# Gated delta rule of a hybrid encoder trunk: substitution through the two 64-row halves of a block in place of one joined inverse

## The chip, the cores and the metric

The kernel runs on one core of a Trainium2 chip. The metric is the device time of one launch in microseconds (us), smaller being better. TensorE multiplies matrices, VectorE and ScalarE work element by element and empty the accumulators (PSUM), GpSimd does a few small operations, and SyncE issues the loads.

## What is computed

Two layers run over 256 positions of width 1024. Each has a gated feed-forward half-step, a mixing stage and a second feed-forward half-step, each followed by a normalisation. The mixing stage projects its input once (`w_in`), runs three groups of heads side by side (differential attention, Mamba-2, gated delta rule) and merges them with one output projection (`w_out`). The change lies in the delta rule, whose core is this part of the reference:

```python
lmat = jnp.where(strict, jnp.einsum('bhcld,bhcsd->bhcls', kb, kc) * decay, 0.0)
imat = jnp.eye(CHUNK, dtype=jnp.float32) + lmat
u = lax.linalg.triangular_solve(imat, vb, left_side=True, lower=True, unit_diagonal=True)
w = lax.linalg.triangular_solve(imat, kb * jnp.exp(gc)[..., None], left_side=True, ...)
...
def step(st, inp):
    u_i, w_i, qd_i, kd_i, a_i, dec_i = inp
    v_new = u_i - jnp.einsum('bhld,bhdv->bhlv', w_i, st)
    o_i = jnp.einsum('bhld,bhdv->bhlv', qd_i, st) + jnp.einsum('bhls,bhsv->bhlv', a_i, v_new)
    st = st * dec_i[..., None, None] + jnp.einsum('bhld,bhlv->bhdv', kd_i, v_new)
    return st, o_i
```

So `v_new` solves a unit lower triangular system. The kernel takes blocks of 128 rows (two of the reference's chunks of 64), so for each of 4 heads and 2 blocks there is one 128 by 128 system, made of two triangles of 64 by 64 on the diagonal and a full 64 by 64 square below them.

## The kernel before

**Tiling.** The 256 positions are two blocks `b` of 128. The large products (feed-forward, `w_in`, `w_out`) split each fp32 operand into a high and a low part and use three TensorE products (lines 221, 222, 228 or 224, and 301). A weight unit is loaded by SyncE into one of 5 `raw` buffers, ScalarE casts the high part (`wh`, line 232), VectorE subtracts for the low part (`wl`, line 233), and 7 `wh` and 7 `wl` buffers hold units ahead of the products. The `w_out` units add into `po`, for `b` = 0 and 1 separately.

**What sets the order.** The program is written out by a planner: `run` emits the weight products one by one, and after each one calls `step`, which advances every generator ("chain") whose due time lies behind the planner's clock. A `yield 0.8` in a chain sets how long it waits, in the planner's estimate, before its next piece is emitted. Each engine then works through its own instructions in the emitted order and waits on semaphores; so a longer or shorter chain moves its neighbours on every engine.

**The delta rule.** `delta` (line 605) forms `LA` for each block: the scaled triangle of keys against keys, and queries against keys. `inverse` (line 743) builds the inverses of the two 64-row triangles of all 8 (block, head) pairs at once, in five levels of block size 2 to 32, kept transposed in `TT` (`T` is the untransposed copy, `gps` and `ups` are the PSUM tiles of a level's two products, `G` the masked copy between). At the last level it also brings `T` up to date for the first half (lines 789 to 793). Then it joins the halves: `X` holds, for the second 64 rows of the result, the columns of the whole inverse; its lower part is copied from `TT` (796), its upper part is made by two further products with a copy between (799 to 808). Back in `delta`, `rhs` is the right side (line 666), and for `b` = 0 and then `b` = 1 eight products into `vnps` give `vnew` (702 to 707): per head one of 64 by 64 for the first half, one over all 128 rows with `X` for the second. From `vnew` come the state `S` (`sps`, only `b` = 0) and the outputs (`ops`). For `b` = 1, `rps` (`S` against keys and queries) first corrects `rhs` (line 685).

**What stands around it.** The Mamba-2 chain (`after_m11`, `after_mz`) runs at the same time: `yps`, `yfps`, then `y` (lines 875 to 908), its squares `msq` on ScalarE (912), the reciprocal root on GpSimd (394, 396), the scaling of `y` on VectorE (920), and transposes into `mTps` on TensorE, which feed the third to sixth `w_out` unit. The delta rule's output `go` takes a similar way (squares 726, sum 728, root, scaling 734, 736) to the last transposes `mTps<-cst,go`, which feed the last two units. The first two units need only the attention's output.

Of the kernel before, what the change touches and what calls it, by code (L numbers as in the profile page):

```python
# [13 lines left out]
ALU = mybir.AluOpType  # L14
# [77 lines left out]
class Kernel:  # L92
# [512 lines left out]
    def delta(self, l, qk, sq):  # L605
        nc = self.nc
        ve = nc.vector
# [22 lines left out]
        LA = []  # L630
# [28 lines left out]
        pk = self.aux(0, "ktok")  # L659
        self.transposes([qk[:, 0, 0:P], qk[:, 2, 0:P]], pk)  # L660
        ve.tensor_tensor(x4, pk[:, 0:256].rearrange("p (h d) -> p h d", h=4), b4(de), op=ALU.mult)
        TT, X = yield from self.inverse(LA)
        lo, hi = slice(0, 64), slice(64, P)
        yield from self.until("gv")
        rhs = self.w([8, 64], "rhs")
# [6 lines left out]
        for b in range(2):  # L672
            if b == 1:

                pr = [self.aux(b, "rps") for _ in range(2)]
                for a in range(2):
                    for j in range(2):
                        for p in range(2):
                            o = slice(64 * p, 64 * p + 64)
                            at = 128 * a + 64 * j  # L680
                            self.mm(pr[p][:, at : at + 64], lhsT=qk[o, 2 * j + a, blk(1)], rhs=S[o, j, :])
                for p in range(2):
                    for j in range(2):
                        hd = 2 * j + p
                        ve.scalar_tensor_tensor(
                            rhs[:, 4 + hd],
                            in0=pr[p][:, 64 * j : 64 * j + 64],
                            scalar=ne[:, hd : hd + 1],
                            in1=rhs[:, 4 + hd],
                            op0=ALU.mult,  # L690
                            op1=ALU.add,
                        )
                for p in range(2):
                    ve.tensor_tensor(
                        oS[:, p::2, :],
                        pr[p][:, 128:256].rearrange("p (j d) -> p j d", j=2),
                        ecs[:, 1, p:4:2].unsqueeze(2).to_broadcast([P, 2, 64]),
                        op=ALU.mult,
                    )
                yield 1.8  # L700
            vnew = self.h(b, [4, 64], "vnew")
            pn = self.aux(b, "vnps")
            for hd in range(4):
                e, c = 4 * b + hd, slice(64 * hd, 64 * hd + 64)
                self.mm(pn[lo, c], lhsT=TT[lo, e, :], rhs=rhs[lo, e, :])
                self.mm(pn[hi, c], lhsT=X[:, e, :], rhs=rhs[:, e, :])
            nc.scalar.copy(vnew.rearrange("p h d -> p (h d)"), pn[:, 0:256])
            yield 0.8
            if b == 0:
                pS = self.aux(b, "sps")  # L710
                for hd in range(4):
                    o = slice(64 * (hd % 2), 64 * (hd % 2) + 64)
                    j = hd // 2
                    self.mm(pS[o, 64 * j : 64 * j + 64], lhsT=x4[:, hd, :], rhs=vnew[:, hd, :])
                nc.scalar.copy(S.rearrange("p j d -> p (j d)"), pS[:, 0:P])
            po = self.aux(b, "ops")
            for hd in range(4):
                self.mm(po[:, 64 * hd : 64 * hd + 64], lhsT=LA[b][:, hd % 2, hd // 2, 1, :], rhs=vnew[:, hd, :])
            out = go[:, 4 * b : 4 * b + 4]
            if b == 0:  # L720
                nc.scalar.copy(out.rearrange("p h d -> p (h d)"), po[:, 0:256])
                yield 0.5
            else:
                ve.tensor_tensor(out, po[:, 0:256].rearrange("p (h d) -> p h d", h=4), oS, op=ALU.add)
# [18 lines left out]
    def inverse(self, LA):  # L743
# [20 lines left out]
        for n, s in enumerate(LEVELS):  # L764
# [21 lines left out]
            for e in range(8):  # L786
                for o in (lo, hi):
                    self.mm(pu[o, 32 * e : 32 * e + 32], lhsT=G[o, e, :], rhs=col1(TT[o, e, :], 1))
            if s == 32:
                for e in range(8):  # L790
                    self.mm(pu[lo, 256 + 32 * e : 288 + 32 * e], lhsT=TT[lo, e, :], rhs=G[lo, e, 0:32])
                dT = pu[lo, 256:512].rearrange("p (h s) -> p h s", h=8)
                ve.tensor_tensor(T[lo, :, 0:32], T[lo, :, 0:32], dT, op=ALU.subtract)
            ve.tensor_tensor(cols(TT, 1), cols(TT, 1), view(pu[:, 0:256]), op=ALU.subtract)
        X = self.w([8, 64], "X")
        nc.scalar.copy(flat(X[hi]), flat(TT[hi]))
        yield 1.2

        pg = self.aux(0, "gps")
        for e in range(8):  # L800
            self.mm(pg[hi, 64 * e : 64 * e + 64], lhsT=LT(e)[lo, hi], rhs=T[lo, e, :])
        G = self.w([8, 64], "G")
        nc.scalar.copy(G[hi].rearrange("p h s -> p (h s)"), pg[hi, :])
        yield 0.8
        pu = self.aux(0, "ups")
        for e in range(8):
            self.mm(pu[lo, 64 * e : 64 * e + 64], lhsT=G[hi, e, :], rhs=TT[hi, e, :])
        ve.tensor_scalar(X[lo], pu[lo, :].rearrange("p (h s) -> p h s", h=8), -1.0, None, op0=ALU.mult)
        yield 0.8
        return TT, X  # L810

    def after_m00(self, l, ps):
        self.xsT = self.big([4, 256], "xsT")
# [403 lines left out]
```

## Time and profile before

| | |
|---|---|
| median of 3 runs | 1095.92 us (1094.84 to 1097.18) |
| the profiled execution | 1094.49 us, span of its instructions 1092.7 us |
| TensorE | busy 1052.6 us, 96% of the span; granted clock 0.996 |
| VectorE, ScalarE, GpSimd | 759.1 us (69%), 600.2 us (55%), 42.0 us (4%) |
| loads | 184.99 MB, mean 169 GB/s |

Columns of the views: a timeline row has the start within the span, the duration, engine, line and operation, result and operands, shapes, and in brackets how long the engine sat idle before it and what released it. A TensorE product of fp32 operands appears as two instructions. TensorE works in a pipeline, so the durations of neighbouring rows overlap: the time that a product takes of the engine is read from start to start. The chain of waits lists, in order of time, the work that ended last at each step; its TensorE pieces are already cut so that they don't overlap. The mixing stages of the two layers lie 536.5 us apart and look alike; the first one is read.

### The profile page before, as it was taken

What the parts mean: (1) busy time and instruction counts of PE and PEld (TensorE: products, weight loads), DVE (VectorE), ACT (ScalarE), POOL (GpSimd) and SP (SyncE); (2) the same over time, 40 slices, a digit from 0 to 9 for tenths busy, and PEclk for the clock granted to TensorE, in tenths of its full rate; (3) what the DMA queues carried; (4) which work ended last, traced back from release to release, by engine and by line L of the source; (5) the groups of instructions that cost most, each with busy time, mean ns of one, the idle gap of its engine ahead of it and who ended that gap; (6) DMA issues with size and microseconds to landing.
All of it is one profiled execution on the core that took longest, in us unless ns stands there. A gap on an engine that the chain in (4) does not pass through costs nothing.

```text
span 1092.7 us, 17702 instructions
## 1 busy us (share of the span) xinstructions
PE 1052.6 (96%) x6397; PEld 896.7 (82%) x6397; DVE 759.1 (69%) x1531; ACT 600.2 (55%) x1284; POOL 42.0 (4%) x51
## 2 busy tenths in 40 slices
PE   6999999999998999999999999999989999999996
PEld 5888878788887788888878888877878877888885
DVE  5767754886867877774587776467967688777644
ACT  6677643487543566664346665436764345666530
POOL 0000000001001100000000000000010110000001
PEclk9999999999999999999999999999999999999999
DMA  9977665661234776666477666637513258666641
GB/s 289 255 210 203 197 195 144 174 193 40 72 104 140 206 214 193 191 188 196 139 225 207 188 193 191 193 98 206 161 40 98 89 159 245 185 192 193 194 134 39
DMA packets 222351, 184.99 MB, mean 169 GB/s; under 512 B 15160, under 2 KB 201912, under 8 KB 222264
## 3 DMA queue, kind: packets, MB, share of 16 engines
q1 hardware_dynamic: 222264, 183.87, 56.9%
q8 instruction: 50, 0.82, 0.3%
q14 instruction: 37, 0.30, 0.1%
HBM read 182.78 MB, written 1.05 MB: 168 GB/s over the span
## 4 chain that ended last, share of the span: by engine, by line
PE 79%; DVE 11%; ACT 3%; DMA 3%; issue 2%; POOL 2%; SPq 0%; DVEq 0%; POOLq 0%; ACTq 0%
PE ps L301 39%; PE po L221 7%; PE po L222 7%; PE po L228 7%; DVE wl L233 4%; PE ps L221 4%; PE ps L222 4%; PE ps L228 3%; DMA raw<-in_ffn_w_gu_dram 2%; PE ups L355 1%; PE gps L355 1%; DMA raw<-in_w_in_dram 1%; ACT wh L232 1%; POOL rsq L396 1%; PE vnps L355 1%
## 5 line engine op out<-in xcount | busy, mean ns | idle before, releaser
L233 DVE TENSOR_TENSOR wl<-raw,wh 128x512 fp32r<-128x512 f32 (+1 forms) x672 | 437.8, 682 | 191.9 <-ACT wh L232 185.3
L232 ACT CAST wh<-raw 128x512 fp32r<-128x512 f32 (+1 forms) x672 | 386.5, 615 | 205.8 <-PE po L228 99.7
L301 PE MATMUL ps<-xT,wh 128*128 128x512 f32 (+1 forms) x1600 | 484.8, 363 | 0.0
L301 PE MATMUL ps<-xT,wl 128*128 128x256 f32 x1376 | 388.4, 282 | 0.0
L301 PEld LDWEIGHTS ps<-xT,wh 128*128 128x128 f32 x1600 | 285.3, 188 | 48.6 <-issue 1.1
L301 PEld LDWEIGHTS ps<-xT,wl 128*128 128x128 f32 x1376 | 260.5, 189 | 0.7 <-issue 0.5
L221 PE MATMUL po<-wh,hT 128*128 128x512 f32 x352 | 137.7, 391 | 0.8 <-DVE hh L457 0.8
L222 PE MATMUL po<-wl,hT 128*128 128x512 f32 x352 | 137.1, 389 | 0.0
L228 PE MATMUL po<-wh,hT 128*128 128x512 f32 x336 | 103.5, 389 | 0.0
L221 PE MATMUL ps<-wh,xT 128*128 128x512 f32 (+2 forms) x256 | 97.1, 379 | 4.3 <-ACT wh L232 4.2
L222 PE MATMUL ps<-wl,xT 128*128 128x512 f32 (+2 forms) x256 | 94.6, 371 | 0.0
L228 PE MATMUL ps<-wh,xT 128*128 128x512 f32 (+2 forms) x224 | 83.6, 374 | 3.4 <-DVE xT L233 3.4
L221 PEld LDWEIGHTS po<-wh,hT 128*128 128x128 f32 x352 | 66.1, 188 | 15.7 <-DVE hh L457 2.2
L222 PEld LDWEIGHTS po<-wl,hT 128*128 128x128 f32 x352 | 66.1, 188 | 13.4
L228 PEld LDWEIGHTS po<-wh,hT 128*128 128x128 f32 x336 | 63.1, 188 | 13.2
L232 ACT CAST hT<-hh 128x256 fp32r<-128x256 f32 x72 | 29.2, 406 | 71.9 <-DVE hh L459 71.9
L221 PEld LDWEIGHTS ps<-wh,xT 128*128 128x128 f32 x256 | 48.5, 190 | 13.6 <-ACT wh L232 5.0
L222 PEld LDWEIGHTS ps<-wl,xT 128*128 128x128 f32 x256 | 48.6, 190 | 8.3 <-DVE wl L233 0.6
L458 ACT ACTIVATE ga<-ga 128x256 f32<-128x256 f32 x72 | 30.1, 418 | 42.4 <-DVE ga L455 42.2
L228 PEld LDWEIGHTS ps<-wh,xT 128*128 128x128 f32 x224 | 42.4, 189 | 11.1 <-DVE xT L233 4.2
L233 DVE TENSOR_TENSOR hT<-hh,hT 128x256 fp32r<-128x256 f32 x72 | 30.5, 424 | 25.8 <-ACT hT L232 25.6
L394 POOL TENSOR_SCALAR rs<-mv 128x1 f32<-128x1 f32 x12 | 6.3, 526 | 790.9 <-DVE mv L378 790.9
(233 smaller groups left out, 970.9 us busy)
## 6 DMA issues: line engine op xcount, KB each, us to landing
raw<-in_ffn_w_gu_dram SPq DMA_DIRECT2D x352, 256.0 KB, 3.5
raw<-in_ffn_w_down_dram SPq DMA_DIRECT2D x88, 512.0 KB, 3.5
raw<-in_w_in_dram SPq DMA_DIRECT2D x40, 512.0 KB, 3.8
raw<-in_w_out_dram SPq DMA_DIRECT2D x16, 512.0 KB, 3.5
raw<-in_w_in_dram SPq DMA_DIRECT2D x24, 256.0 KB, 3.9
g<-in_ln_g_dram SPq DMA_DIRECT2D x6, 512.0 KB, 5.5
b<-in_ln_b_dram SPq DMA_DIRECT2D x6, 512.0 KB, 5.6
x<-in_x_dram SPq DMA_DIRECT2D x4, 256.0 KB, 3.4
```

The source lines that it names most:

```text
L221: mm(p, lhsT=xh, rhs=wh, start=start, stop=False)
L222: mm(p, lhsT=xh, rhs=wl, start=False, stop=False)
L228: mm(p, lhsT=xl, rhs=wh, start=False, stop=False)
L232: self.nc.scalar.copy(hi, src)
L233: self.nc.vector.tensor_tensor(lo, src, hi.bitcast(F32), op=ALU.subtract)
L301: self.nc.tensor.matmul(to, lhsT=a, rhs=r, start=first and n == 0, stop=end and n == len(mms) - 1, skip_group_check=True,)
L355: self.nc.tensor.matmul(out, lhsT=lhsT, rhs=rhs, start=start, stop=stop)
L394: nc.gpsimd.tensor_scalar(t, ap, mul, add, op0=ALU.mult, op1=ALU.add)
L396: nc.gpsimd.tensor_tensor(r, t, self.neghalf[:, :n], op=ALU.pow)
L458: nc.scalar.activation(a, a, AF.Silu)
```

## The change

`inverse` stops at `TT`. The update of `T` at the last level and everything on `X` are gone: per layer 8 products into `ups`, 8 into `gps`, 8 into `ups`, two VectorE and two ScalarE operations, and three yields. In `delta` each block's eight products and one copy become three groups of four products of 64 by 64, with a step on another engine after each: first half from `TT`, copied to `vnew[lo]` by ScalarE; the square `LA[lo, hi]` against that, subtracted from `rhs[hi]` by VectorE; second half from `TT`, copied to `vnew[hi]` by ScalarE.

```diff
-        TT, X = yield from self.inverse(LA)
+        TT = yield from self.inverse(LA)
...
-            for hd in range(4):
-                e, c = 4 * b + hd, slice(64 * hd, 64 * hd + 64)
+            flat = lambda t, o: t[o].rearrange("p h d -> p (h d)")
+            heads = [(hd, 4 * b + hd, slice(64 * hd, 64 * hd + 64)) for hd in range(4)]
+            for hd, e, c in heads:
                 self.mm(pn[lo, c], lhsT=TT[lo, e, :], rhs=rhs[lo, e, :])
-                self.mm(pn[hi, c], lhsT=X[:, e, :], rhs=rhs[:, e, :])
-            nc.scalar.copy(vnew.rearrange("p h d -> p (h d)"), pn[:, 0:256])
+            nc.scalar.copy(flat(vnew, lo), pn[lo, 0:256])
+            yield 0.8
+            pn = self.aux(b, "vnps")
+            for hd, e, c in heads:
+                self.mm(pn[hi, c], lhsT=LA[b][lo, hd % 2, hd // 2, 0, hi], rhs=vnew[lo, hd, :])
+            r2 = rhs[hi, 4 * b : 4 * b + 4, :]
+            ve.tensor_tensor(r2, r2, pn[hi, 0:256].rearrange("p (h d) -> p h d", h=4), op=ALU.subtract)
+            yield 0.8
+            pn = self.aux(b, "vnps")
+            for hd, e, c in heads:
+                self.mm(pn[hi, c], lhsT=TT[hi, e, :], rhs=rhs[hi, e, :])
+            nc.scalar.copy(flat(vnew, hi), pn[hi, 0:256])
             yield 0.8
...
-            if s == 32:
-                for e in range(8):
-                    self.mm(pu[lo, 256 + 32 * e : 288 + 32 * e], lhsT=TT[lo, e, :], rhs=G[lo, e, 0:32])
-                dT = pu[lo, 256:512].rearrange("p (h s) -> p h s", h=8)
-                ve.tensor_tensor(T[lo, :, 0:32], T[lo, :, 0:32], dT, op=ALU.subtract)
             ve.tensor_tensor(cols(TT, 1), cols(TT, 1), view(pu[:, 0:256]), op=ALU.subtract)
-        X = self.w([8, 64], "X")
-        nc.scalar.copy(flat(X[hi]), flat(TT[hi]))
-        yield 1.2
-
-        pg = self.aux(0, "gps")
-        for e in range(8):
-            self.mm(pg[hi, 64 * e : 64 * e + 64], lhsT=LT(e)[lo, hi], rhs=T[lo, e, :])
-        G = self.w([8, 64], "G")
-        nc.scalar.copy(G[hi].rearrange("p h s -> p (h s)"), pg[hi, :])
-        yield 0.8
-        pu = self.aux(0, "ups")
-        for e in range(8):
-            self.mm(pu[lo, 64 * e : 64 * e + 64], lhsT=G[hi, e, :], rhs=TT[hi, e, :])
-        ve.tensor_scalar(X[lo], pu[lo, :].rearrange("p (h s) -> p h s", h=8), -1.0, None, op0=ALU.mult)
-        yield 0.8
-        return TT, X
+        return TT
```

Since the yields change, the planner emits other work around the delta rule. On every engine the instructions up to the last level's `ups` products and from the first block's normalisation on stand as before. The first group of block 0 now stands 9 weight products behind the last `ups`, the second behind `cbps`, the third 30 weight products later; `yps` and `yfps` follow behind it. `rhs<-gv,nk` on VectorE moves ahead of a `wl` step.

TensorE, second block, before: the last pair of `vnps` products, then the output products `ops`, then the first `w_out` product (`po`); `ps` is the projection's last part.

```order
L355 MATMUL vnps_3575<-rhs_3479,TT_2849 64x64
L355 MATMUL vnps_3575<-rhs_3479,X_3385 64x64
L222 MATMUL ps_3634<-wl_3410,xT_2107 128x256
L228 MATMUL ps_3634<-wh_3409,xT_2107 128x256
L221 MATMUL ps_3634<-wh_3409,xT_2107 128x256
L222 MATMUL ps_3634<-wl_3410,xT_2107 128x256
L355 MATMUL ops_3617<-vnew_3574,LA_2818 128x64 x4
L228 MATMUL ps_3634<-wh_3409,xT_2107 128x256
L221 MATMUL ps_3634<-wh_3409,xT_2107 128x256
L222 MATMUL ps_3634<-wl_3410,xT_2107 128x256
L224 MATMUL ps_3634<-wh_3409,xT_2107 128x256
L221 MATMUL po_3710<-wh_3471,mT_2490 128x512
```

TensorE, second block, now: the end of the first group, four weight products, the second group.

```order
L355 MATMUL vnps_3528<-rhs_3376,TT_2849 64x64 x3
L222 MATMUL ps_3618<-wl_3413,xT_2107 128x256
L228 MATMUL ps_3618<-wh_3412,xT_2107 128x256
L221 MATMUL ps_3618<-wh_3412,xT_2107 128x256
L222 MATMUL ps_3618<-wl_3413,xT_2107 128x256
L355 MATMUL vnps_3542<-vnew_3527,LA_2818 64x64 x4
L228 MATMUL ps_3618<-wh_3412,xT_2107 128x256
```

TensorE, second block, now, seven weight products later: the third group and `ops`.

```order
L224 MATMUL ps_3618<-wh_3412,xT_2107 128x256
L221 MATMUL po_3694<-wh_3455,mT_2490 128x512
L355 MATMUL vnps_3563<-rhs_3376,TT_2849 64x64 x4
L222 MATMUL po_3694<-wl_3456,mT_2490 128x512
L221 MATMUL po_3695<-wh_3455,mT_2490 128x512
L222 MATMUL po_3695<-wl_3456,mT_2490 128x512
L228 MATMUL po_3694<-wh_3455,mT_2490 128x512
L355 MATMUL ops_3601<-vnew_3527,LA_2818 128x64 x4
```

The third group and `ops` now stand behind the first `w_out` products; the last transposes `mTps<-cst,go` have 38 `w_out` products ahead of them where they had 33.

ScalarE, second block, before: from the copy of `go` of block 0 to the squares of `y`.

```order
L721 COPY go_3483<-ops_3515 128x256
L707 COPY vnew_3574<-vnps_3575 128x256
L912 ACTIVATE msq_3587,mss_3585<-y_3428 128x256
L912 ACTIVATE msq_3589,mss_3585<-y_3428 128x256
L912 ACTIVATE msq_3592,mss_3585<-y_3428 128x256
L912 ACTIVATE msq_3594,mss_3585<-y_3428 128x256
L726 ACTIVATE sq_616_3623<-go_3483 128x512
```

ScalarE, second block, now (lines 707 and 718 are the copies of the two halves).

```order
L232 CAST wh_3717<-raw_3461 128x512 x2
L707 COPY vnew_3527<-vnps_3528 64x256
L232 CAST wh_3752<-raw_3525 128x512
L718 COPY vnew_3527<-vnps_3563 64x256
L232 CAST wh_3752<-raw_3525 128x512
L903 ACTIVATE msq_3571,mss_3569<-y_3438 128x256
```

The squares stand behind both copies of the block and behind the two halves of one weight unit's cast, which stood behind them before. On VectorE the second block's subtraction (line 713) stands between the `yfps` step of `y` and the two operations that finish `y`.

## Rows read from the trace of the kernel before

**Rows 1.** Page, part 1: busy time (share), instructions, of TensorE.

```profile
PE 1052.6 (96%) x6397; PEld 896.7 (82%) x6397; DVE 759.1 (69%) x1531; ACT 600.2 (55%) x1284; POOL 42.0 (4%) x51
```

**Rows 2.** Waits of TensorE, whole run: us in total, times, longest.

```profile
PE xps L237 <- DVE x L383: 3.4, 4, 1.1
...
PE mTps L237 <- DVE y L920: 3.2, 2, 1.6
PE mTps L237 <- DVE go L736: 3.1, 2, 1.6
```

**Rows 3.** Windows of 4 us: length, busy per engine, clock, DMA share, GB/s.

```profile
336.00:340.00 4.00, 2.42 (x16) 2.10 (x16) 3.97 (x8) 1.40 (x3) 1.23 (x1) 1.00 0.41 131
344.00:348.00 4.00, 2.44 (x13) 1.95 (x13) 4.00 (x8) 1.45 (x3) 0.00 (x0) 1.00 0.17 51
348.00:352.00 4.00, 4.00 (x20) 3.29 (x19) 2.54 (x6) 1.03 (x3) 0.00 (x0) 1.00 0.99 311
```

**Rows 4.** Chain that ended last, first layer: start us, us, what.

```profile
300.32 1.05 PE ups L355 x32
...
308.10 1.98 PE ups L355 x48
...
312.98 1.07 PE gps L355 x16
...
316.27 0.84 PE ups L355 x12
...
318.14 0.37 PE ups L355 x4
...
322.65 2.05 PE vnps L355 x16
...
329.30 0.51 PE vnps L355 x4
...
330.36 1.55 PE vnps L355 x12
```

**Rows 5.** The same chain, from the squares of y to the last transposes.

```profile
332.21 1.72 ACT msq L912 x8
...
336.03 2.66 DVE y L920 x4
...
345.78 0.63 PE mTps L237 x4
```

**Rows 6.** Timeline of TensorE: start us, us, line, operation [idle before].

```profile
331.57 0.33 PE L355 MATMUL vnps<-rhs,X 128*64 128x64 f32 x2
331.83 0.39 PE L222 MATMUL ps<-wl,xT 128*128 128x256 f32 x1
...
332.40 1.06 PE L355 MATMUL ops<-vnew,LA 128*128 128x64 f32 x8
333.28 0.37 PE L228 MATMUL ps<-wh,xT 128*128 128x256 f32 x1
...
333.84 0.39 PE L221 MATMUL po<-wh,mT 128*128 128x512 f32 x1
334.07 0.39 PE L222 MATMUL po<-wl,mT 128*128 128x512 f32 x1
...
337.65 0.41 PE L237 MATMUL mTps<-cst,y 128*128 128x128 f32 x2 [1.58 <-DVE y L920]
```

**Rows 7.** Timeline of ScalarE, same columns.

```profile
331.94 0.37 ACT L707 COPY vnew<-vnps 128x256 f32<-128x256 f32 x1 [4.35 <-PE vnps L355]
...
335.09 1.14 ACT L232 CAST wh<-raw 128x512 fp32r<-128x512 f32 x2
```

**Rows 8.** Timeline of VectorE, same columns.

```profile
310.11 0.41 DVE L793 TENSOR_TENSOR T<-T,ups 64x256 f32<-64x256 f32 x1 [1.82 <-PE ups L355]
...
313.36 2.49 DVE L868 TENSOR_TENSOR ex<-ex,CB 128x512 f32<-128x512 f32 x4
...
329.60 1.28 DVE L908 TENSOR_TENSOR y<-y,sz 128x512 f32<-128x512 f32 x2
```

## The prediction

> **What bounds the kernel now.** I read the page's first part, then the waits of TensorE, the windows of the mixing stage, and last its chain of waits. TensorE is busy 96% of the span [rows 1], so by default an instruction taken off it is worth its own time. The exceptions are the places where it waits. Over both layers the transposes of `y` wait 3.2 us and those of `go` 3.1 us, two waits each, or 1.6 us per layer and place; each normalisation costs 1.1 us at most [rows 2]. The windows around the first two have only 2.4 of 4 us busy on TensorE, at full granted clock, and the next window is full again [rows 3]. The chain names what is late there: the second block's `vnps` products, then ScalarE's squares of `y`, GpSimd's root, VectorE's scaling of `y`, and from there to the transposes of `go` [rows 4, 5]. So the stage has two limits: up to the second block's `vnew` TensorE's own work, behind it a chain over four engines. Time taken off TensorE moves the start of that chain, and only that is won.
>
> **The change, part by part.** All for one layer; the other repeats it.
>
> *Removed from TensorE.* The last level's `ups` pieces take 1.98 us for 48 instructions, where a level without the update of `T` takes 1.05 us for 32: 0.93 us goes. The join's `gps` takes 1.07 us, its `ups` 0.84 + 0.37 us, the two blocks' `vnps` 2.05 and 0.51 + 1.55 us [rows 4]. Sum 7.32 us.
>
> *Added to TensorE.* Six groups of four 64 by 64 products, eight instructions each. The nearest row is the join's `gps`, the same shape, all products out of one half: 1.07 us for 16, 0.067 us each [rows 4], so 0.53 us a group and 3.2 us in all. From below it is bounded by `ups`, where the halves alternate: 1.05 us for 32, 0.26 us a group [rows 4]; from above by today's `vnps`, 2.05 us for 16, 0.128 us each, 1.03 us a group [rows 4]. I take 0.53, since shape and half agree. Net, TensorE gets rid of 4.1 us, with bounds of 1.1 and 5.7.
>
> Why do today's `vnps` instructions cost twice as much as those of `gps`? In them a 64-row product and a 128-row one alternate, in `gps` all have one shape [rows 4, 6]. The Trainium skill, TensorEngine Tiling (Array Packing), section Tiling Modes, says that a change of tiling mode drains the engine. That agrees with the row and would let the alternation's cost go; but it speaks against the change as well, because six short groups each enter and leave the small mode between full products. By the rule the difference of 0.061 us per instruction, some 0.12 us per change of mode, would come twice per group, 1.5 us a layer, and the sum would be some 3 us less for the whole kernel. The first full product behind `ops` starts its neighbour no earlier than today, so I keep the row's price.
>
> *Added waits.* Each group is followed by a step on another engine on which the next depends. Such a hand-over is in the trace: the last `vnps` pair starts at 331.57 us and `ops`, behind the copy, at 332.40: 0.83 us [rows 6]. Four weight products of 256 columns that stand between take 332.40 - 331.83 = 0.57 us [rows 6]. In the second block again four stand between first and second group, so TensorE waits about 0.26 us. Between second and third stand seven and one of 512 columns, over 1 us, between third and `ops` four of 512 columns, some 0.9 us: covered. In the first block `cbps` covers the first hand-over; before the third group stand 30 weight products of 0.12 us, 3.6 us, against VectorE's subtraction of 0.41 us behind the 2.49 us of `ex` times `CB` [rows 8]: covered with about 1 us to spare. If that cover were gone, each hand-over would cost its 0.83 us.
>
> *Off TensorE.* VectorE loses the update of `T` and the negation into `X` and gets two subtractions of 64 rows, 0.41 us by the row for `T` [rows 8]. ScalarE loses two copies and has four of `vnew` for two, 0.37 us each if a half takes as long as the whole [rows 7]. Both engines have idle time here; I cost this at nothing except for the queue in front of the squares, next. Behind the first block's subtraction are queued `wl` steps needed much later. Behind the second block's stand the last operations on `y`: one addition and the two halves of the product with `sz`, 0.6 us each as half of 1.28 [rows 8]. The third group can't start before that subtraction is done, so the first half of `y` is ready at most 1.2 us behind the group's start.
>
> *When the chain starts.* Today the stretch from the last `ups` pieces at 308.10 to the first `w_out` product at 333.84 takes 25.74 us [rows 4, 6]. Take off 7.32, and the 0.88 us of `ops` (332.40 to 333.28 [rows 6]), which now stands behind; add five groups, 2.65, and the wait of 0.26: 20.45 us, so the first `w_out` product comes at 328.55. One product of 0.23 us (333.84 to 334.07 [rows 6]) later the third group starts at 328.8; its last pair of instructions starts 0.47 - 0.07 us on, at 329.2, and ends after another 0.33 [rows 6]: 329.5. ScalarE copies 0.37 us, as today 0.04 us behind the end [rows 6, 7], until 329.9, then casts half a weight unit, 0.57 us as half of 1.14 [rows 7], and begins the squares at 330.5. (`y` is there at 328.8 + 1.2 = 330.0.) Today they begin at 332.21 [rows 5]. The chain starts **1.7 us earlier**.
>
> *What the chain keeps.* From the squares to the transposes of `y` are 337.65 - 332.21 = 5.44 us [rows 5, 6], from the scaling of `y` at 336.03 to the transposes of `go` at 345.78 another 9.75 us [rows 5]. Neither stretch is touched: as many VectorE operations stand in each, only `mT` and `wl` steps of about equal length change places. So both sets of transposes come 1.7 us earlier. TensorE waits there longer than today, and does five more `w_out` products before the transposes of `go` (38 for 33): 5 x 0.23 = 1.1 us that no longer comes behind. From there on TensorE waits for nothing until the normalisation, and that starts with the last of these products. Won: 1.7 + 1.1 = **2.8 us a layer**, 5.7 us in all by the unrounded numbers. As a check: of 4.1 us less work, 0.26 goes into the hand-over and about 1.0 into longer waits at the transposes.
>
> **The rivals.**
>
> *A, TensorE's work is the whole limit.* If the squares can begin still earlier, the waits stay at 3.1 us and all 4.1 us count: 8.2 us, 1086.3 on the profiled execution, 1087.7 on the median. For it: 96%. Against: ScalarE comes to the squares only behind the copy and the cast.
>
> *B, the small groups are dear.* At 0.128 us an instruction [rows 4] each is 0.50 us dearer; five lie in front of the chain, 2.5 us, and 2.8 turns into 0.3 us a layer: 1095.2. For it: the rule on the change of mode goes the same way. Against: `gps`, with other products around it.
>
> *C, the loads don't follow.* The window behind the transposes runs the DMA engines at a share of 0.99 [rows 3]. Its loads are freed by VectorE steps that come 1.7 us earlier, not 2.8; if they set the start of the next feed-forward, 1.7 us a layer is left, 3.4 in all: 1092.5. Against: the waits of TensorE in this stage name VectorE [rows 2], none a load.
>
> *D, slower: the hand-overs lie bare.* The triangular substitution is now three steps in a row where there was one. If ScalarE or VectorE is held by earlier work at each of the six hand-overs, TensorE, which works in order, stands 0.83 us [rows 6] six times: 5.0 us, 4.7 more than counted. The layer then ends 1.9 us later than today, 3.8 us in all: 1099.7. It decides from 3.1 us of such waits per layer. For it: the first block's subtraction stands behind 2.49 us of other work [rows 8], and the second `vnew` copy behind a cast that waits until TensorE is through with an older unit. Against: the order puts 0.5 us and more of products into each gap. That the change doesn't do what it says I leave out: the order shows the products gone.
>
> **How the numbers follow.** The profiled execution took 1094.49 us; less 5.7 it is 1088.8. It lies 1.4 us under the median of 1095.92, so I put the forecast on the median: **1090.2 us**. Chances: forecast 0.56, A 0.12, B 0.14, C 0.09, D 0.09. The range has to reach from A to B and leaves out most of D: 1086.8 to 1095.3. About 0.2%, 2.2 us, is what a measurement of this kernel can tell from no change. Faster than 1093.7 come out the forecast but for its tail, A and C: 0.76. Same: B and that tail, 0.15. Slower: D, 0.09.
>
> **What would show it.** In the profile of the changed kernel: TensorE's busy time down by some 8 us; groups of eight `vnps` instructions in 0.53 us each (B: 1 us); the first `w_out` product of the first layer near 328.5; the squares of `y` near 330.5, 0.6 us behind the second copy, not behind `y` itself; waits at the transposes of `y` and `go` of about 2 us each rather than 1.6 (A: unchanged); the last normalisation of the stage some 2.8 us earlier (C: 1.7, with a wait for a load in front of it). Waits of TensorE in front of `vnps` products of more than 0.3 us would speak for D. The forecast is wrong above all if a group costs more than its row says, or if `y` is not ready when ScalarE is.

## The result, and the profile after

Medians of four runs each: 1089.53 us (1088.08 to 1090.70) for the changed kernel against 1095.38 for the kernel before, ratio 0.994 with a 95% interval of 0.9927 to 0.9954: 5 to 8 us faster. The forecast was 1090.2 us, 5.7 us less. The profiled execution took 1090.7 us.

The chain of waits of the changed kernel, first layer (start, duration, what):

```profile
308.46 1.05 PE ups L355 x32
...
327.63 0.60 PE vnps L355 x8
...
329.50 0.62 PE vnps L355 x8
...
331.16 1.61 ACT msq L903 x8
332.85 0.35 POOL rs L394
333.28 1.34 POOL rsq L396
334.65 2.66 DVE y L911 x4
...
339.64 1.65 POOL rsq L396
...
344.03 0.63 PE mTps L237 x4
...
364.65 0.64 PE xps L237 x4
```

The last line is the stage's last normalisation handing over to the next feed-forward. Before it stood here:

```profile
367.54 0.64 PE xps L237 x4
```

Spans of different executions begin with other delays, so I measure from the last level's `ups`, 308.10 before [rows 4] and 308.46 now: 59.44 us to this `xps` before, 56.19 now. The stage is 3.25 us shorter, in the second layer as well, 6.5 us in all. That lies inside the interval; the medians differ by 5.85 us.

ScalarE in front of the squares (`msq`), in the timeline of the changed kernel:

```profile
330.14 0.37 ACT L718 COPY vnew<-vnps 64x256 f32<-64x256 f32 x1 [0.21 <-PE vnps L355]
330.54 0.62 ACT L232 CAST wh<-raw 128x512 fp32r<-128x512 f32 x1
331.06 0.41 ACT L903 ACTIVATE msq<-y 128x256 f32<-128x256 f32 x1
```

Copy, half cast, squares, as the prediction had them: 331.06 less 308.46 is 22.60 us behind `ups`, for 24.11 before [rows 4, 5], 1.51 earlier. TensorE's waits, all layers (total, times, longest), to be held against [rows 2]:

```profile
PE ktok L237 <- DVE LA L645: 4.4, 2, 2.2
...
PE mTps L237 <- DVE y L911: 2.9, 2, 1.5
...
PE mTps L237 <- DVE go L747: 2.6, 2, 1.3
```

The waits at the two sets of transposes got shorter, 3.2 to 2.9 and 3.1 to 2.6 us. The prediction had them growing.

TensorE's busy time fell by only 2.2 us in this execution, for 64 instructions (32 products) fewer:

```profile
PE 1050.4 (96%) x6333; PEld 893.3 (82%) x6333; DVE 759.3 (70%) x1531; ACT 600.6 (55%) x1284; POOL 40.7 (4%) x51
```

### The profile page after: what moved, and what is told of

Read it like the earlier page. It is cut to its first block, busy times and chain, and to the rows that moved or that the text cites. A ratio compares the mean times of both kernels' runs of the same rounds, so it can differ in the third digit from the quotient of the medians.

```text
span 1088.9 us, 17572 instructions
## 1 busy us (share of the span) xinstructions
PE 1050.4 (96%) x6333; PEld 893.3 (82%) x6333; DVE 759.3 (70%) x1531; ACT 600.6 (55%) x1284; POOL 40.7 (4%) x51
## 3 DMA queue, kind: packets, MB, share of 16 engines
HBM read 182.78 MB, written 1.05 MB: 169 GB/s over the span
## 4 chain that ended last, share of the span: by engine, by line
PE 82%; DVE 9%; ACT 3%; DMA 2%; issue 2%; POOL 2%; SPq 1%; POOLq 0%; DVEq 0%; ACTq 0%
PE ps L301 42%; PE po L221 7%; PE po L222 7%; PE po L228 7%; PE ps L221 4%; PE ps L222 4%; DVE wl L233 3%; PE ps L228 3%; DMA raw<-in_w_in_dram 1%; ACT wh L232 1%; PE ups L355 1%; PE gps L355 1%; POOL rsq L396 1%; DMA raw<-in_ffn_w_gu_dram 1%; PE vnps L355 1%
## 5 line engine op out<-in xcount | busy, mean ns | idle before, releaser
L221 PEld LDWEIGHTS ps<-wh,xT 128*128 128x128 f32 x256 | 48.7, 190 | 12.4 <-ACT wh L232 3.8
L228 PEld LDWEIGHTS ps<-wh,xT 128*128 128x128 f32 x224 | 42.7, 191 | 11.1 <-DVE xT L233 4.2
L457 DVE TENSOR_TENSOR hh<-ps,hh 128x256 f32<-128x256 f32 x72 | 30.2, 419 | 8.4 <-ACT hh L456 8.4
```

What stands on the lines that cost most here:

```text
L221: mm(p, lhsT=xh, rhs=wh, start=start, stop=False)
L228: mm(p, lhsT=xl, rhs=wh, start=False, stop=False)
L457: nc.vector.tensor_add(hh, up[:, 0:256], hh)
```

## The experiments

Ratios are to the kernel before, timed on the same chip in turn. "Stage" is the distance from the last level's `ups` to the last `xps` of the first layer (before: 59.44 us), "squares" that to the first `msq` (before: 24.11).

| kernel | ratio (95%) | in us | squares | stage, difference |
|---|---|---|---|---|
| changed kernel | 0.994 (0.9927 to 0.9954) | -8.0 to -5.0 | 22.60 | -3.25 |
| the same again | 0.9952 (0.9940 to 0.9964) | -6.6 to -3.9 | 22.60 | -3.26 |
| before, regrouped | 0.9987 (0.9976 to 0.9999) | -2.6 to -0.1 | 22.57 | -1.54 |
| before, no join | 0.9946 (0.9934 to 0.9959) | -7.2 to -4.5 | 22.08 | -3.48 |
| changed, copy on VectorE | 0.9971 (0.9960 to 0.9982) | -4.4 to -2.0 | 22.93 | -2.15 |
| changed, 12 products more | 0.9974 (0.9965 to 0.9983) | -3.8 to -1.9 | 24.10 | -1.70 |
| changed, no root | 0.9935 (0.9919 to 0.9952) | -8.9 to -5.3 | 22.60 | -2.30 |
| changed, two yields less | 0.9991 (0.9978 to 1.0003) | -2.4 to +0.3 | 25.10 | -0.60 |
| changed, reordered | 0.9913 (0.9899 to 0.9928) | -11.1 to -7.9 | 22.60 | -4.28 |
| reordered, gate on VectorE | 0.9903 (0.9887 to 0.9919) | -12.4 to -8.9 | 22.61 | -5.34 |
| changed, gate on VectorE | 0.9931 (0.9915 to 0.9946) | -9.3 to -5.9 | 22.60 | -3.88 |

**The changed kernel again.** No edit.

> The changed kernel a second time, nothing edited. The first pair of traces puts the last x projection 3.25 us earlier per layer against the start of the solve's last level, 6.5 us over both, but the two profiled spans differ by only 3.8 us and TensorE's busy time by only 2.2 us. Theory: the missing 2.7 us are execution to execution variation of the feed-forward stretch, so this interval lies again at 5 to 6.5 us below before, the 3.25 us per layer show again within 0.1 us, and TensorE's busy time may fall anywhere from 2 to 8 us below before. Rival: the change itself makes the feed-forward slower (TensorE clocked lower behind the new order); then the feed-forward products are again near 399 ns each against 391 ns, and the busy time is again only about 2 us lower.

Measured: 1089.32 us, and the stage is the same to 0.01 us. Busy time now 5.4 us below before:

```profile
PE 1047.2 (97%) x6333; PEld 891.7 (82%) x6333; DVE 758.9 (70%) x1531; ACT 600.0 (55%) x1284; POOL 40.7 (4%) x51
```

What differed between the two executions shows in the windows (stretch, length, busy time and instructions of PE, PEld, DVE, ACT, POOL, granted clock, DMA share, GB/s) of the second layer's feed-forward; first execution, then second:

```profile
620.00:640.00 20.00, 20.00 (x115) 17.34 (x114) 14.04 (x29) 13.12 (x31) 0.00 (x0) 1.00 0.64 187
```

```profile
620.00:640.00 20.00, 20.00 (x118) 17.62 (x117) 14.98 (x30) 12.92 (x29) 0.00 (x0) 1.00 0.66 189
```

Same work, same granted clock, 115 instructions for 118: 3 in 118 over a pass of about 100 us is some 2.5 us. Passes at either rate turn up in the runs of several kernels, the kernel before regrouped among them (115 in each window from 400 to 480 but one of 116), so the rival (the change slows the feed-forward) falls. What selects the rate I could not see.

**The kernel before, products regrouped.** In each block:

```diff
             for hd in range(4):
                 e, c = 4 * b + hd, slice(64 * hd, 64 * hd + 64)
                 self.mm(pn[lo, c], lhsT=TT[lo, e, :], rhs=rhs[lo, e, :])
+            for hd in range(4):
+                e, c = 4 * b + hd, slice(64 * hd, 64 * hd + 64)
                 self.mm(pn[hi, c], lhsT=X[:, e, :], rhs=rhs[:, e, :])
```

> The kernel before, with one thing moved: in each block of heads the four 64 by 64 products with the lower half's inverse come first, then the four 128 by 64 products with the joined inverse; before, they alternate. Same products, same joined inverse. Theory (the alternation of the two shapes is what made these sixteen products dear: 2.05 us per block of 16 instructions, 0.128 each, against 0.075 in the groups of the changed kernel): a block falls from 2.05 to 1.0 to 1.1 us, TensorE's work ahead of the squares falls by about 2 us per layer, and as the squares stand behind the second block they begin some 1.5 to 2 us earlier; 2 to 4 us off the whole. So part of what the change won would have nothing to do with the join. Rival (the products of 64 rows are dear by their own shape, or each block waits for its right-hand sides anyway): a block stays within 0.2 us of 2.05 and the time within 0.5 us of before.

The chain of waits:

```profile
322.21 1.21 PE vnps L355 x16
...
328.02 0.25 PE vnps L355 x2
...
328.83 1.11 PE vnps L355 x14
...
330.23 1.72 ACT msq L914 x8
```

A block falls from 2.05 us [rows 4] to 1.21 and 1.36, 0.076 to 0.085 us an instruction for 0.128. The squares come 1.54 us earlier and the stage ends 1.54 us earlier. The blocks' gain is 4.11 - 2.57 = 1.54 us as well. So the alternation of a 64-row with a 128-row product was the dear part. The prediction cites the Trainium skill, TensorEngine Tiling (Array Packing), section Tiling Modes, for a drain at a change of tiling mode; the trace agrees with it, but shows only that the order costs time, not that it is a drain. Two added lines give nearly half of what the change gives in the stage. The timed gain of 1.3 us falls short of the expected 2 to 4, and of the stage's 3.1 us over both layers, which lie half a microsecond outside its interval; that difference is not explained.

**The kernel before, without the join.** Left out: the update of `T`, `gps`, `ups` and the copy between; the upper half of `X` is filled with `-T` in place of the joined part, and the planner's clock is advanced as if the products stood there.

```diff
-                for e in range(8):
-                    self.mm(pu[lo, 256 + 32 * e : 288 + 32 * e], lhsT=TT[lo, e, :], rhs=G[lo, e, 0:32])
...
+                self.clock += 8 * 0.213
...
-        for e in range(8):
-            self.mm(pg[hi, 64 * e : 64 * e + 64], lhsT=LT(e)[lo, hi], rhs=T[lo, e, :])
...
-        for e in range(8):
-            self.mm(pu[lo, 64 * e : 64 * e + 64], lhsT=G[hi, e, :], rhs=TT[hi, e, :])
-        ve.tensor_scalar(X[lo], pu[lo, :].rearrange("p (h s) -> p h s", h=8), -1.0, None, op0=ALU.mult)
+        ve.tensor_scalar(X[lo], T[lo], -1.0, None, op0=ALU.mult)
```

> The kernel before, without the join: the update of the upper half's last 32 columns, the two products that form the off-diagonal quarter of the joined inverse and the copy between them are left out, and the upper rows of the joined inverse are filled from what is there without them (so what is computed is wrong); the order table's clock is advanced as if they stood there. The two substitution blocks are as before. Theory (the join is TensorE work on the one path: 1.07 + 0.84 + 0.37 and one x32 of the last ups, some 3 us per layer by the rows of the kernel before): the blocks, the squares and the last x projections come 2.5 to 3.2 us earlier per layer, 5 to 6.4 us in all. Rival (the sixteen products wait for the right-hand sides, not for the inverse): under 1.5 us in all, the wait moving to the products ahead.

```profile
319.07 2.05 PE vnps L355 x16
...
329.33 1.71 ACT msq L903 x8
```

The first block comes 2.7 us earlier against `ups`, the squares 2.0 (2.5 to 3.2 were expected), the stage ends 3.48 earlier (second layer 3.24). The theory stands: the join lay on the path. The stage gains more than the squares because GpSimd's two `rs` steps took 0.20 us in this layer for 0.58 (0.76 together, more on this below) and because more `w_out` products stand in front of the last transposes (0.69). The two halves of the old design were not taken out together; if their prices add up, some 3.4 us a layer are won without the join, up to 1.5 more without the alternation, and the six groups take back what lies between that sum and 3.25.

**The changed kernel, one copy moved to VectorE.**

```diff
-            nc.scalar.copy(flat(vnew, hi), pn[hi, 0:256])
+            (ve.tensor_copy if b else nc.scalar.copy)(flat(vnew, hi), pn[hi, 0:256])
```

> The changed kernel, with one copy moved: in the second block the upper half of vnew goes from PSUM to SBUF on VectorE instead of ScalarE. In the changed kernel the squares start at 331.06, 0.62 behind the half cast which stands behind this copy on ScalarE, although the first half of y is there at 329.98. Theory (ScalarE's queue ahead of the squares sets their start): the squares start 0.4 to 1 us earlier per layer and the last x projections follow one to one: 0.8 to 2 us off the whole. Rival A (TensorE's own work is what is left: it waits only 2.9 and 2.6 us for two transposes each): half of it, 0.4 to 1 us. Rival B (VectorE is busy with the scaling of y there, and the copy pushes that back): no gain, or up to 0.8 us slower.

Rival B had the sign right. ScalarE's timeline, then VectorE's:

```profile
330.83 0.42 ACT L903 ACTIVATE msq<-y 128x256 f32<-128x256 f32 x1 [0.94 <-DVE y L899]
```

```profile
329.58 0.43 DVE L718 COPY vnew<-vnps 64x256 f32<-64x256 f32 x1 [0.72 <-PE vnps L355]
330.04 1.29 DVE L899 TENSOR_TENSOR y<-y,sz 128x512 f32<-128x512 f32 x2
```

VectorE works in order: the copy waits 0.72 us for the third group, and the product of `y` with `sz` stands behind it. VectorE was not busy with the scaling of `y`, as rival B had it, but held up in front of the product. The squares are 0.33 us later, not earlier, and now wait for `y`. What follows cost more than that: against the changed kernel the stage loses 1.10 us, in the second layer 1.66, more than the 0.8 us in all that the rival allowed. TensorE's timeline and windows:

```profile
335.90 0.44 PE L237 MATMUL mTps<-cst,y 128*128 128x128 f32 x2 [2.02 <-DVE y L911]
```

```profile
334.00:338.00 4.00, 2.10 (x12) 1.72 (x13) 3.63 (x6) 0.84 (x2) 1.56 (x2) 0.93 0.45 131
338.00:342.00 4.00, 4.00 (x13) 3.18 (x12) 2.18 (x7) 1.47 (x3) 2.21 (x2) 0.64 0.29 82
```

Behind a wait of 2.02 us the granted clock falls to its lower level, and the window has 13 products where the changed kernel has 19.

**Twelve products more.**

```diff
-            for hd, e, c in heads:
-                self.mm(pn[hi, c], lhsT=TT[hi, e, :], rhs=rhs[hi, e, :])
+            for again in range(4 if b == 0 else 1):
+                for hd, e, c in heads:
+                    self.mm(pn[hi, c], lhsT=TT[hi, e, :], rhs=rhs[hi, e, :])
+            self.clock -= 12 * 0.213 if b == 0 else 0
```

> The changed kernel with twelve more products per layer: the third group of the first block (four products of 64 by 64, 0.60 us in its trace) is issued four times over, with the same result in the same place; the order table's clock is set back by the same amount. Theory (TensorE's work ahead of the chain to the end counts one to one): some 1.8 us per layer, 3.6 us on the whole, and the squares begin 1.5 to 1.8 us later against the solve's last level. Rival (the chain over VectorE, GpSimd and ScalarE sets the end and TensorE has 2.9 and 2.6 us of slack at the transposes): under 1 us on the whole, the waits at the transposes smaller by as much.

```profile
316.54 2.00 PE vnps L355 x32
```

They cost 2.00 - 0.60 = 1.40 us, not 1.8; the squares move by 1.50 and the stage by 1.55 us. That this is nearly one to one is in part chance, because the order changed too: 0.46 us of weight products moved behind the second block's third group, which so comes only 0.94 us later (329.13 less 307.15, for 329.50 less 308.46), and ScalarE's cast of a whole weight unit, not of half of one, now stands between the copy and the squares. What it shows is the theory: TensorE's work up to there, with the cast behind it, sets the start of the chain.

**Without the root.** `y` is scaled by the sum of squares itself, so GpSimd's root is left out.

```diff
-        r = self.rsqrt(b, ss, 1.0 / 256, EPS, 4)
+        r = ss
```

> The changed kernel without GpSimd's inverse root of the mean square of y: y is scaled by the sum itself (so what is computed is wrong); the sum of squares and the scaling stay. Theory (the chain from the squares to the transposes of y is what TensorE waits for there, 2.9 us in two layers): the chain is about 1 to 1.8 us shorter per layer, the wait of 1.45 us at the first transpose of y goes, and the last x projections come 1 to 1.5 us earlier per layer, 2 to 3 us in all. Rival (TensorE's work ahead of the transposes is the bound, and what it does not wait for y it waits for the gate product behind): the wait moves from the transposes of y to those of the product with the gate, and the whole gains under 1 us.

```profile
331.21 1.69 DVE L911 SCALAR_TENSOR_TENSOR y<-y,mss,mnw 128x256 f32<-128x256 f32 x4 [0.37 <-ACT msq L903]
```

```profile
343.19 0.93 PE L237 MATMUL mTps<-cst,go 128*128 128x128 f32 x4 [2.07 <-DVE go L747]
```

The transposes of `y` come 3.0 us earlier and without a wait, those of `go` only 0.45, with a wait of 2.07, and behind it the clock falls again (0.67 in the window from 342 to 346). The wait moved, as the rival says. The stage is 0.95 us longer than in the changed kernel while the timed runs are not slower; its 4.6 us over both layers lie 0.7 us outside the timed interval. The profiled execution was the slowest of the four (1091.47 us, granted clock 0.990; the others 1086.36 to 1088.81 at 0.993 to 0.998), so the fall of the clock need not be in the others. That stays open.

**Two yields less.**

```diff
-            yield 0.8
             pn = self.aux(b, "vnps")
...
-            yield 0.8
```

> The changed kernel without the two places inside a block where the order table may put other work between the three steps: the second and third group of each block then stand closer behind the copy that they read, with less of other products in between, and the work that stood there comes elsewhere. Theory (the hand-over of 0.83 us from a group over the copy back to TensorE is covered by the products between; where it is not, TensorE waits): waits of 0.3 to 0.8 us appear at up to four groups per layer and the time rises by 1 to 4 us. Rival (TensorE's work is the bound and the products moved from there fill other waits): within 1 us of the changed kernel.

Some 4 to 6 us slower than the changed kernel (the theory gave 1 to 4), but not by the theory's mechanism: no wait stands in front of any group. Without the yields the planner put `yfps` behind the groups, `y` was late, and TensorE waited there instead:

```profile
339.58 0.63 PE L237 MATMUL mTps<-cst,y 128*128 128x128 f32 x3 [3.86 <-DVE y L909]
```

What a bare hand-over costs was therefore not measured.

**The order behind the squares.** In the changed kernel the sum of `go`'s squares (`gss`, L739) is queued on VectorE behind the scaling of `y`, though its input is there at 333.3 and VectorE stands idle for 0.90 us until the first root is done.

```diff
         r = self.rsqrt(0, gs, 1.0 / 64, EPS, 8)
+        yield 6
         ve.tensor_mul(r, r, rq)
-        yield 3.5
...
         r = self.rsqrt(b, ss, 1.0 / 256, EPS, 4)
+        yield 0.1
```

> The changed kernel with the order behind the squares changed: the scaling of y on VectorE is issued one step later and the product of the inverse root with rq six units later, so that the reduction of the gated output's squares (L739, 0.67) stands in the 0.90 us for which VectorE waits for GpSimd ahead of the scaling of y, and the second root can begin some 3 us earlier; TensorE finds the transposes of y behind 17 products instead of 15 and those of the gated output behind 35 instead of 38. Nothing is computed otherwise. Theory (what is left ahead of the transposes is two chains in series on VectorE, of which the second starts late only because it is queued behind the first): the wait of 1.31 at the gated output's transposes goes, that at y's falls from 1.46 to about 1.1, the last x projections come 1.3 to 1.7 us earlier per layer, 2.6 to 3.4 in all. Rival A (the reduction and its two products push back the scaling of y by 0.3 to 0.9): y's wait grows and half is left, 1 to 1.5 us in all. Rival B (the wait at y reaches 2 us, and TensorE's clock falls behind it as in three of the runs so far): no gain or up to 1 us slower.

1085.66 us, faster than both kernels. VectorE's timeline, GpSimd's, and TensorE's waits in this stage:

```profile
331.75 0.68 DVE L739 TENSOR_REDUCE gss<-sq 128x8 f32<-128x512 f32 x1
332.73 1.49 DVE L912 SCALAR_TENSOR_TENSOR y<-y,rsq,mnw 128x256 f32<-128x256 f32 x1 [0.30 <-POOL rsq L396]
```

```profile
332.67 1.27 POOL L1034 TENSOR_TENSOR gw<-gw,gnw 128x512 f32<-128x512 f32 x1
...
335.32 2.35 POOL L396 TENSOR_TENSOR rsq<-rs,neghalf 128x8 f32<-128x8 f32 x1
```

```profile
PE mTps L237 <- DVE y L912: 1.0, 1, 1.0
PE mTps L237 <- DVE go L747: 0.8, 1, 0.8
```

The sum fills the idle time, the scaling starts no later. The stage gains 1.03 us instead of the 1.3 to 1.7 expected, and 0.8 us of the wait at `go` is left, because GpSimd's second root took 2.35 us for 1.65 before. The first scaling of `y` took 1.49 us, with GpSimd's product of 1.27 us beside it, and the next 0.47. That led to the last two runs.

**The gate's product on VectorE**, with the reordering and without.

```diff
-            nc.gpsimd.tensor_tensor(gw, gw, self.gnw[l].unsqueeze(1).to_broadcast([P, 8, 64]), op=ALU.mult)
+            nc.vector.tensor_tensor(gw, gw, self.gnw[l].unsqueeze(1).to_broadcast([P, 8, 64]), op=ALU.mult)
```

> The reordered changed kernel of the run before, with one operation on another engine: the product of the gate with its norm weights (128x512) goes from GpSimd to VectorE, behind the scaling of y. In the runs so far the four scalings of y take 2.66 us while that product runs on GpSimd (1.25 to 1.27 us, started 0.06 us ahead of them), and 1.69 us in the run without the root, where it does not run beside them. Theory (VectorE's scaling of y stands still while GpSimd's product runs): the scalings take 1.6 to 1.7 us, y's transposes find their operand 1.0 us earlier and wait for nothing or 0.3 us instead of 1.0, the second root starts about 1 us earlier, the transposes of the gated output wait under 0.3 us instead of 0.8; the last x projections come 1.2 to 1.8 us earlier per layer, 2.4 to 3.6 us in all. Rival (the scalings are slow for another reason, their first one waiting for the root's result): they still take 2.6 us in total, VectorE has 0.68 more to do, and the time is the same or up to 1.4 us longer.

> The changed kernel as it was recorded, with only that one operation moved from GpSimd to VectorE; the order is otherwise unchanged, the product stands on VectorE ahead of the last step before the second root. Theory (VectorE stands still beside GpSimd's product): the scalings of y take 1.6 to 1.7 us instead of 2.66, the wait at y's transposes falls from 1.46 to about 0.4, but the second chain gains only 0.4 us because 0.6 of VectorE's work now lies ahead of its root, so the wait at the gated output's transposes grows from 1.31 to 1.7 to 1.9 us: 0.4 us per layer, 0.8 in all. Rival (slow for another reason): scalings unchanged, both chains 0.6 later, 1.2 us slower in all.

Without the reordering all four scalings together (VectorE's timeline):

```profile
332.88 1.67 DVE L911 SCALAR_TENSOR_TENSOR y<-y,rsq,mnw 128x256 f32<-128x256 f32 x4 [0.90 <-POOL rsq L396]
```

1.67 us for 2.66: VectorE had stood still beside GpSimd's product. The wait at `y` falls to 0.48, that at `go` grows to 1.66, about as expected, and the stage gains 0.63 us (0.4 expected). With the reordering the wait at `y` is gone, but 0.7 at `go` is left where under 0.3 was expected; the stage is 1.06 us shorter than with the reordering alone (1.2 to 1.8 expected) and 5.34 us shorter than before, and the kernel takes **1083.48 us**, the best here. The second root, in that kernel:

```profile
334.36 2.96 POOL L396 TENSOR_TENSOR rsq<-rs,neghalf 128x8 f32<-128x8 f32 x1
```

It ends 1.50 us behind the last of the `wl` steps that VectorE ran beside it (335.13 + 0.69 = 335.82), in the kernel of the run before as well (335.49 + 0.68 = 336.17 and 337.67). So GpSimd seems to stand still too; no run takes those steps away from beside it.

## Why the prediction was right

*What bounds the stage*: TensorE up to the second block, then a chain over four engines. Products added and products left out moved the chain's start, and the chain's own work paid when it was shortened. Right.

*Work removed*: the regrouped kernel and the one without the join bear out both the alternation's price and the join's. *Work added* was undersized: 0.60 to 0.62 us a group, and 0.26 + 0.49 us where weight products split one, not 0.53; 0.075 us an instruction, the same as in the first block of the regrouped kernel. Six groups take 3.77 us, net 3.55 for the 4.1 forecast. Rival B's 1.03 us is excluded. The work around the groups grew as well. The stage got 3.25 us shorter, and 0.4 of that are shorter waits (6.3 us over both layers before, 5.5 now), so TensorE's work fell by 2.9 us a layer, not 3.55. Read from start to start, the 73 instructions of `w_out` in the stage take 17.7 us for 17.1, those of the transposes 1.25 for 1.05. One place is the first weight product behind a group, here 0.32 us in the chain for 0.12 elsewhere:

```profile
328.24 0.32 PE ps L228
```

This stood behind `vnps` and `gps` before too, so part of it cancels. The 0.65 us a layer between 3.55 and 2.9 is less than the 1.5 us that the prediction works out from the Trainium skill's rule on tiling modes; how much of it is a change of mode, no run separates.

*The hand-over wait* of 0.26 us did not come. TensorE's timeline of the changed kernel:

```profile
327.35 0.28 PE L222 MATMUL ps<-wl,xT 128*128 128x256 f32 x1
327.56 0.68 PE L355 MATMUL vnps<-vnew,LA 64*64 64x64 f32 x8
```

The second group follows its neighbour directly. The prediction's own rows had no wait either: its 0.83 us runs from the start of the last `vnps` pair, the pair itself takes 331.83 - 331.57 = 0.26 us of that, and the four weight products the other 0.57 [rows 6]. So the pair's time was counted once in its group and once more as a wait, and by these rows a bare hand-over would leave TensorE idle for 0.57 us at most, not 0.83. Rival D has no place in the trace.

*Start of the chain*: expected 1.7 us earlier, 1.51 found. The five groups ahead took 3.15 us for 2.65, and the wait of 0.26 that did not come gave about half of that back; that two misses cancelled in part was luck.

*"What the chain keeps"* was the step that failed, in our favour. Squares to `y`'s transposes took 5.12 us (336.18 less 331.06) for 5.44, scaling to `go`'s transposes 9.38 for 9.75. The transposes of `y` in the changed kernel (TensorE), then GpSimd's first step of each root before, which now took 0.35 and 0.20 us:

```profile
336.18 0.83 PE L237 MATMUL mTps<-cst,y 128*128 128x128 f32 x4 [1.47 <-DVE y L911]
```

```profile
334.00 0.58 POOL L394 TENSOR_SCALAR rs<-mss 128x4 f32<-128x4 f32 x1 [41.68 <-ACT msq L912]
...
340.73 0.58 POOL L394 TENSOR_SCALAR rs<-gss 128x8 f32<-128x8 f32 x1 [3.50 <-DVE gss L730]
```

The prediction had said that only `mT` and `wl` steps of about equal length change places in these stretches. That exchange is what differs at the second root: VectorE ran a `wl` step beside its `rs` before, and an `mT` step now. VectorE before; then VectorE and GpSimd of the changed kernel:

```profile
340.56 0.68 DVE L233 TENSOR_TENSOR wl<-raw,wh 128x512 fp32r<-128x512 f32 x1
```

```profile
339.18 0.68 DVE L233 TENSOR_TENSOR mT<-mTps,mT 128x512 fp32r<-128x512 f32 x1
```

```profile
339.35 0.20 POOL L394 TENSOR_SCALAR rs<-gss 128x8 f32<-128x8 f32 x1 [3.51 <-DVE gss L741]
```

Beside `wl`, `rs` ends 0.07 us behind the end of the `wl` step (341.31 and 341.24); beside `mT` it is through long before the `mT` step is. The kernel without the join has the `mT` step there and 0.20 us, the changed kernel with only the gate moved a `wl` step and 0.57. No run exchanges these two steps alone. So the transposes of `go` came 2.11 us earlier, not 1.7, and with the 1.14 of five more `w_out` products the stage gained 3.25 for 2.8. Of these 3.25 us, 1.51 are the chain's earlier start; the rest, 0.60 and 1.14, hangs on the order that the planner happened to write, and the 0.60 the prediction had not foreseen.

*The check* was wrong in sign: waits of about 2 us at each place were forecast, 1.5 and 1.3 found. TensorE arrives there about 1.7 us earlier, no more than the chain's head start, since it got rid of less work than forecast, and the chain shortened besides. *Busy time down by some 8 us* was too much for the same reason: it fell by 5.7 us by the stage, by 5.4 on the page of the second execution. The first execution's 2.2 had a feed-forward pass that ran 2 to 3% slower, so one page's busy time does not resolve such a change.

*Rival C*: no wait for a load stands in the stage, and its end moved by more than the chain's start. *Rival A* had its sign in the profile, waits that do not grow, nearer than the forecast had; its 8.2 us did not come, because there were only 2.9 us a layer to win. That TensorE's work is not the whole limit is shown by the last three runs, where the stage got 0.6 to 2.1 us shorter with the same products on TensorE.

The stage's 6.5 us lie inside the first interval and at the edge of the second (6.6 to 3.9); the medians gain 5.9 and 5.3 us, so some of it may be given back elsewhere, where I did not find it. So part of how near the forecast of 5.7 us came to the timed 5.9 is luck. One candidate is the wait at `ktok`, 2.8 us before and 4.4 after. It varies from run to run (1.1 to 4.4): the wait is 2.2 us at full clock and 0.5 to 0.8 where the granted clock had dipped in front of it (0.59 in the window from 264 to 268 before), so the longer wait alone is no loss.

## What to carry to other kernels

Price a group of small products by the order it stands in, not only by its shape: putting products of one shape together cost two lines and gave nearly half of this change's gain in the stage (less in the timed runs). Where a chain over several engines follows TensorE's work, look for what is queued in front of each link and what runs beside it on VectorE and GpSimd; two such edits together won another 2.1 us a layer in the stage, about two thirds of what the algorithm did. Judge an edit of a few microseconds by distances inside its stage, over two executions, next to the timed interval: the span and the busy time of one execution scatter as much as the edit is worth.

## What was not expected of the hardware

- *VectorE and GpSimd hold each other up.* Four scalings of `y` take 2.66 us beside GpSimd's 128x512 product and 1.67 to 1.69 without it; a root of 8 columns takes 1.64 us, and 2.35 or 2.96 beside VectorE's `wl` steps. The Trainium skill, SBUF — State Buffer, section SBUF: two separate sides, says that the two share a pair of ports and that whichever starts first holds it for its whole instruction; for VectorE it names the instructions with two SBUF inputs, such as the scaling and `wl`, or in a two-port mode. The trace agrees: 1.0 us of the product's 1.25 to 1.27, and `rs` takes 0.58 us beside a `wl` step but 0.20 beside an `mT` step, one of whose two inputs lies in PSUM. The 0.35 us of the first `rs` fits too, but no run isolates it.
- *The clock after a wait.* Behind waits of 2.02, 2.07 and 3.86 us at these transposes TensorE's granted clock fell to the lower level, with `w_out` products 0.43 us apart instead of 0.23; behind 1.47, 1.58 and 1.85 us it stayed at 1.00. The length of a wait alone does not tell: behind a wait of 2.21 us at `ktok` it stayed at 1.00 in the second layer of the kernel before, and fell in the first layer of the changed kernel (0.73 and 0.85 in the two windows of 4 us from 268). A chain made shorter in one place and longer in another can pay twice.
- *Two rates of the feed-forward* at the same granted clock, 115 or 118 instructions in 20 us, cause open.
